# Output projection and second feed-forward projection as 2x2 blocks in seven products of sums

## The chip, the cores and the metric

The kernel runs on one core of a Trainium2 chip. The metric is the device time in microseconds of one execution, from the first to the last instruction and what the launch puts around them. The engines have names of their own in the profile: PE is TensorE (PEld its weight loads), DVE is VectorE, ACT is ScalarE, POOL is GpSimd, SP is SyncE, which here only issues loads and stores.

## The reference

One layer of an encoder with 512 tokens and 1024 features, all in float32:

```python
h = x @ w_in                       # columns: q | k | v | latents | rope key | gate A | gate B
y_a = neighbourhood_attention_2d(q, k, v, rpb) @ w_branch_na      # 8 heads
y_b = latent_attention(q_lat, kv_lat, k_rope, ...) @ w_branch_mla # 8 heads
merged = sigmoid(g_a + b_a) * y_a + sigmoid(g_b + b_b) * y_b
x = layer_norm(DN_ALPHA * x + merged @ w_out, ln1_g, ln1_b)       # (512,1024) @ (1024,1024)
gate, up = split(x @ w_ffn_in)                                    # 2 x 2816 columns
x = layer_norm(DN_ALPHA * x + (silu(gate) * up) @ w_ffn_out, ln2_g, ln2_b)   # (512,2816) @ (2816,1024)
```

The change concerns the two products `merged @ w_out` and `(silu(gate) * up) @ w_ffn_out`, and through its memory the parts between them.

## The kernel before, in words

**Precision.** A float32 operand is kept as two tiles, a rounded part `hi` (ScalarE copies it, L79) and the remainder `lo` (VectorE subtracts, L80); together they are one "split". A product is then three matmuls in a row, hi by hi, hi by lo, lo by hi (`mm3`, L102 to L104). The left operand has 128 contraction rows and 128 tokens, the right one 128 contraction rows and up to 512 columns.

**Stages in program order.** Latents and attentions with other projections between them; gate A, branch A and the merge (L580 to L596); the output projection (L682) with its layer norm and the transposes of the result (L693, split in L701 and L702); the first feed-forward part (22 hidden units of 128, L719 to L732); the second projection with the last layer norm and the stores (L735).

**A projection** (`project_out`, L601) has the eight accumulators of its 512 x 1024 result in the eight PSUM banks (`ACC`, L599): four row blocks of 128 tokens, called 0 to 3 below, by two halves of 512 columns. It goes over the contraction blocks `k` (8 in the output projection, 22 in the second); each block's weights (128 x 1024, 512 KB) are loaded by SyncE into one of two buffers `raw` and split into `hi` and `lo` of 512 columns, of which there are four each; then follow 24 matmuls. The last blocks (`tail`: 4 and 6) are kept back and done row block by row block (L622 to L634), so that the row blocks are complete one after another. Some blocks of the tail are split earlier, into slots of their own (`early`; `V` tiles in the output projection, `X` tiles in the second). The last 256 columns of the last row block have an accumulator of their own.

**The norm** (`residual_norm`, L644) adds the accumulators to the residual rows (L647), takes mean and variance (L655, L657), has 1/sqrt computed on GpSimd (L127, L129), and applies scale and shift in two operations for each half (L660, L664). The residual rows sit in eight tiles `OT`; GpSimd loads them (L674) and multiplies them by ALPHA (L675) while the projection runs, and once more after the transposes (L705).

**What sets the order.** The program is written in the order of the stages, and a scheduler of the framework arranges each engine's instructions anew when the program is built; on the chip each engine runs its own list strictly in order and waits by semaphores. SyncE and GpSimd issue their transfers in that order too. Tiles come from rings (`BUFS`, L64): a tile's name is its ring, so a new `raw` waits until the readers of the `raw` two back are done.

## Time and profile before

| What | Value |
|---|---|
| Time, median of 3 runs | 742.45 us (740.47, 742.45, 743.89) |
| Span of the profiled execution | 739.6 us |
| Granted clock of TensorE, mean over the span | 0.998 |
| Attentions up to the output projection | 0 to 322.9 us, PE busy 317.19 |
| Output projection | 322.9 to 366.4 us |
| Last norms, transposes, first unit of the feed-forward | 366.4 to 382.9 us |
| First feed-forward part, other units | 382.9 to 611.4 us |
| Second projection, up to the last matmul | 611.4 to 731.5 us |
| Last norm and stores | 731.5 to 739.6 us |

The span runs from the first to the last instruction of one execution that the profiler recorded; the time of a run also holds what lies around the span, so the two differ by a few microseconds, and runs differ among themselves. In the rows that follow, an entry such as `lo<-raw,hi 128x512` reads: tile `lo` written from tiles `raw` and `hi`, 128 partitions by 512 elements; `x144` is the number of instructions in a group, behind it their busy time in us and the mean of one in ns, and behind the second bar the idle time of the engine just before them with what ended most of it. A row of the timeline begins with its start and its duration in us, and ends with the wait ahead of it in square brackets.

### The profile page before, as it was taken

The page shows a single profiled execution, that of the slowest core. Times are in us where ns is not written, and L with a number is a line of the kernel's source. Part 1 is how long each engine was busy: PE and PEld are TensorE (multiplying, and loading weights), DVE is VectorE, ACT ScalarE, POOL GpSimd, SP SyncE. Part 2 cuts the span into 40 slices and gives each one's busy share as a digit, 9 for nine tenths or more (in the row PEclk, how much of TensorE's full clock was granted, in tenths as well). Part 3 has the DMA queues.
Part 4 walks back from the last instruction along what each step waited for, and adds up shares of the span by engine and source line. Part 5 has one row for each costly group of instructions (what it writes and reads, how often), then busy time and mean ns, then how long its engine had stood idle before and what let it go on. Part 6 is the DMA issues. An engine that isn't in the chain of part 4 may idle for free.

```text
span 739.6 us, 9589 instructions
## 1 busy us (share of the span) xinstructions
PE 725.1 (98%) x3606; PEld 610.9 (83%) x3606; DVE 390.6 (53%) x649; ACT 313.0 (42%) x608; POOL 106.6 (14%) x214
## 2 busy tenths in 40 slices
PE   8999999999999999999999999999999999999995
PEld 7988888886898788888798888888888888888884
DVE  5657667667847847454973333344334334322265
ACT  5567657667655654332143333333333333322200
POOL 0312211324404340040320000000000000000011
PEclk9999999999999999999999999999999999999999
DMA  7311030113314252266022323323233234432111
GB/s 262 134 58 56 32 101 30 57 48 103 108 58 139 90 185 86 85 204 195 0 86 86 112 88 92 109 86 111 88 97 103 86 109 150 144 111 86 57 50 65
DMA packets 22207, 72.91 MB, mean 99 GB/s; under 512 B 2833, under 2 KB 3729, under 8 KB 22161
## 3 DMA queue, kind: packets, MB, share of 16 engines
q1 hardware_dynamic: 20880, 68.11, 29.3%
q0 software_dynamic: 1280, 4.20, 1.8%
q8 instruction: 28, 0.46, 0.3%
q14 instruction: 19, 0.15, 0.1%
HBM read 70.20 MB, written 2.10 MB: 98 GB/s over the span
## 4 chain that ended last, share of the span: by engine, by line
PE 90%; DVE 4%; POOL 2%; ACT 1%; issue 1%; DMA 1%; SPq 0%; POOLq 0%; DVEq 0%; ACTq 0%
PE psA L103 22%; PE psA L104 22%; PE psA L102 22%; PE psS L104 3%; PE psS L102 3%; PE psS L103 3%; PE psT L426 2%; PE psT L103 2%; PE psT L102 2%; PE psT L104 2%; POOL Q L503 1%; PE psV L438 1%; PE psV L439 1%; PE psV L103 1%; PE psV L102 1%
## 5 line engine op out<-in xcount | busy, mean ns | idle before, releaser
L80 DVE TENSOR_TENSOR lo<-raw,hi 128x512 fp32r<-128x512 f32 (+1 forms) x214 | 148.6, 700 | 207.5 <-ACT hi L79 206.3
L79 ACT ACTIVATE hi<-raw 128x512 fp32r<-128x512 f32 (+1 forms) x214 | 133.3, 628 | 258.0 <-PE psA L103 130.0
L102 PE MATMUL psA<-X,hi 128*128 128x512 f32 (+1 forms) x560 | 217.3, 388 | 0.0
L103 PE MATMUL psA<-X,hi 128*128 128x512 f32 (+1 forms) x560 | 215.3, 384 | 0.0
L104 PE MATMUL psA<-X,lo 128*128 128x512 f32 (+1 forms) x560 | 215.3, 384 | 0.0
L104 PEld LDWEIGHTS psA<-X,lo 128*128 128x128 f32 x560 | 105.3, 188 | 20.5
L103 PEld LDWEIGHTS psA<-X,hi 128*128 128x128 f32 x560 | 105.5, 188 | 19.0
L102 PEld LDWEIGHTS psA<-X,hi 128*128 128x128 f32 x560 | 105.5, 188 | 18.8
L127 POOL TENSOR_SCALAR s<-s 128x1 f32<-128x1 f32 (+1 forms) x12 | 5.4, 453 | 378.6 <-DVE s L657 378.3
L503 POOL TENSOR_SCALAR Q<-SP,s 64x192 f32<-64x192 f32 (+2 forms) x64 | 34.5, 539 | 44.8 <-DVE s L497 40.3
L415 POOL TENSOR_SCALAR SP<-SP,s 128x512 f32<-128x512 f32 x32 | 24.3, 759 | 82.1 <-DVE s L414 80.8
L175 DVE SCALAR_TENSOR_TENSOR PT<-psT,PT 128x512 fp32r<-128x512 f32 (+1 forms) x48 | 31.1, 662 | 5.6 <-ACT PT L174 5.5
L729 DVE TENSOR_TENSOR M<-M,psA 128x512 f32<-128x512 f32 x22 | 15.1, 688 | 34.1 <-PE psA L104 32.4
L174 ACT ACTIVATE PT<-psT 128x512 fp32r<-128x512 f32 (+1 forms) x48 | 26.9, 578 | 13.7 <-PE psT L426 6.2
L412 ACT ACTIVATE SP<-psS,s 128x512 f32<-128x512 f32 x32 | 22.0, 688 | 10.9 <-DVE s L409 10.9
L102 PE MATMUL psA<-OT,hi 128*128 128x512 f32 x64 | 25.6, 400 | 0.0
L104 PE MATMUL psA<-OT,lo 128*128 128x512 f32 x64 | 25.0, 391 | 0.0
L103 PE MATMUL psA<-OT,hi 128*128 128x512 f32 x64 | 25.0, 390 | 0.0
L409 DVE TENSOR_REDUCE s<-psS 128x1 f32<-128x512 f32 x32 | 21.7, 680 | 0.6 <-PE psS L104 0.3
L372 DVE TENSOR_TENSOR M<-psV,M 64x512 f32<-64x512 f32 x16 | 11.0, 689 | 18.8 <-ACT M L371 18.7
L102 PE MATMUL psA<-hi,X 128*128 128x256 f32 (+1 forms) x56 | 18.1, 326 | 0.7 <-ACT hi L79 0.7
L371 ACT ACTIVATE M<-psV 64x512 f32<-64x512 f32 x16 | 9.5, 594 | 21.1 <-PE psV L531 15.6
(434 smaller groups left out, 1251.3 us busy)
## 6 DMA issues: line engine op xcount, KB each, us to landing
raw<-in_wfi_dram SPq DMA_DIRECT2D x44, 512.0 KB, 3.6
raw<-in_wfo_dram SPq DMA_DIRECT2D x22, 512.0 KB, 3.6
raw<-in_wgb_dram SPq DMA_DIRECT2D x8, 512.0 KB, 3.4
raw<-in_wqk_dram SPq DMA_DIRECT2D x8, 512.0 KB, 3.3
raw<-in_wga_dram SPq DMA_DIRECT2D x8, 512.0 KB, 3.4
raw<-in_wout_dram SPq DMA_DIRECT2D x8, 512.0 KB, 4.2
B<-in_nabias_dram SPq DMA_DIRECT2D x8, 384.0 KB, 3.1
raw<-in_wv_dram SPq DMA_DIRECT2D x4, 512.0 KB, 3.5
```

What stands on the lines that cost most here:

```text
L79: act.activation(hi, raw, AF.Copy)
L80: dve.tensor_tensor(out=lo, in0=raw, in1=f(hi), op=ALU.subtract)
L102: pe.matmul(o, lhsT=ah, rhs=bh, start=first, stop=False)
L103: pe.matmul(o, lhsT=ah, rhs=bl, start=False, stop=False)
L104: pe.matmul(o, lhsT=al, rhs=bh, start=False, stop=last)
L174: act.activation(hi, psv, AF.Copy if isinstance(scale, float) else AF.Identity, scale=scale)
L175: dve.scalar_tensor_tensor(out=lo, in0=psv, scalar=scale, in1=f(hi), op0=ALU.mult, op1=ALU.subtract)
L409: dve.reduce_max(out=mx, in_=s, axis=AX.X, negate=True)
L412: act.activation(pr[:, :512], s, AF.Exp, bias=mx, accum_out=sm)
L415: pool.tensor_scalar(out=pr[:, :512], in0=pr[:, :512], scalar1=rc, scalar2=0.0, op0=ALU.mult, op1=ALU.add)
L503: pool.tensor_scalar(out=pr[m_, dst:dst + c1 - c0], in0=ev[m_, i, c0:c1], scalar1=rc[m_, i:i + 1], scalar2=0.0, op0=ALU.mult, op1=ALU.add)
L729: dve.tensor_tensor(out=sg, in0=sg, in1=os[1], op=ALU.mult)
```

## The change

Two contraction blocks and the two halves of the rows and of the columns make a product of 2x2 blocks. `A11, A12` are the rows 256 to 511 of the left operand in contraction block 0 and 1 of a pair, `A21, A22` the rows 0 to 255; `B11, B12, B21, B22` are the weights of 128 x 512 (first index the contraction block, second the column half). Instead of eight block products, seven are made, from sums of blocks:

- 1: A11 B11, and into the same accumulator A12 B21
- 5: (A21 - A22) (B11 + B12), and into the same accumulator (A12 - A11 + A21 - A22) B22
- 7: (A11 - A21) (B12 + B22), and into the same accumulator A22 (B11 + B12 + B22 + B21)
- 6: (A11 - A21 + A22) (B11 + B12 + B22)

The additions at the end give each product its sign. Every product has two row blocks of 128, so four products in each of two row blocks fill the eight banks (`acc`).

The work of a projection is done in three sweeps over the pairs (4 in the output projection, 11 in the second). **Sweep 1** makes the first four products above. For each pair it loads 1 MB into one of two buffers `w` (the weights lie in memory as `B11 | B12 | B22 | B21`), splits the two left sums (`ca`, `cb`) and `B11`, and lets GpSimd make three sums: `t13` (L651, 1024 columns, split into `u13`), `t2` (L654, split into `u2`), and the sum of all four, which overwrites the left sums that are used up (L657). Between sweeps 1 and 2, corrections are added from the accumulators into the residual tiles (L665 to L674). **Sweep 2** adds A22 by the sum of all four to product 7, after which row blocks 0 and 1 are complete and get their norm. **Sweep 3** loads `B22 | B21` once more and finishes products 1 and 5 with the row blocks 2 and 3; the last 2 or 4 pairs are held back and done row block by row block.

The sums of the left blocks are made by VectorE (`combine`, four operations of 256 columns for each pair). The merged values and the hidden units are therefore kept unsplit. All tiles whose rings belong to the attentions are given back behind the merge (`first.close()`), and a second set of rings (`w`, `x0`, `x1`, `rw`) takes their place.

```diff
-    BUFS = dict(raw=2, hi=4, lo=4, X=8, QK=12, V=6, PT=10, SP=6, OT=10, G=8, M=3, Q=4, B=2, s=24, t=3)
+    BOTH = dict(raw=2, hi=4, lo=4, X=8, OT=10, G=8, M=3, s=24, t=3)
+    PHASES = (dict(QK=12, V=6, PT=10, SP=6, Q=4, B=2), dict(w=2, x0=11, x1=11, rw=4))
...
-        dve.tensor_tensor(out=g, in0=g, in1=gates[fc], op=ALU.add)
-        mh = st("QK", [P, T], F32R)
-        ml = st("PT", [P, T], F32R)
-        split(g, mh, ml)
-        merged.append((mh, ml))
+        dve.tensor_tensor(out=gates[fc], in0=g, in1=gates[fc], op=ALU.add)
+        merged.append(gates[fc])
+    first.close()
+    pools.append(ctx.enter_context(tc.tile_pool(name="second", bufs=1, reuse_waits="tile")))
...
+    def combine(a11, a12, a21, a22, s1, s3, s2):
+        dve.tensor_tensor(out=s1, in0=a21, in1=a22, op=ALU.subtract)
+        dve.tensor_tensor(out=s3, in0=a11, in1=a21, op=ALU.subtract)
+        dve.tensor_tensor(out=s2, in0=a11, in1=s1, op=ALU.subtract)
+        dve.tensor_tensor(out=a21, in0=a12, in1=s2, op=ALU.subtract)
...
+        for j, (c1, a22, a12, s4) in enumerate(pairs):
+            w = st("w", [P, 2048])
+            nc.sync.dma_start(out=w, in_=src[j])
+            ca = split_new(ctag, c1[:, 0:512], 512)
+            cb = split_new(ctag, c1[:, 512:1024], 512)
+            b11 = st("hi", [P, 512], F32R), st("lo", [P, 512], F32R)
+            split(w[:, 0:512], *b11)
+            t13 = st("raw", [P, 1024])
+            pool.tensor_tensor(out=t13, in0=w[:, 0:1024], in1=w[:, 512:1536], op=ALU.add)
+            u13 = split_new(wtags[0], t13, 1024)
+            t2 = st("M", [P, 512])
+            pool.tensor_tensor(out=t2, in0=w[:, 0:512], in1=t13[:, 512:1024], op=ALU.add)
+            u2 = st("hi", [P, 512], F32R), st("lo", [P, 512], F32R)
+            split(t2, *u2)
+            pool.tensor_tensor(out=c1[:, 0:512], in0=t2, in1=w[:, 1536:2048], op=ALU.add)
+            parts = [(1, (ca, 0), (b11, 0)), (5, (ca, 256), (u13, 0)), (7, (cb, 0), (u13, 512)), (6, (cb, 256), (u2, 0))]
+            for q, a, b in parts if j < n - 1 else [parts[i] for i in (2, 0, 1, 3)]:
+                for i in range(2):
+                    product(q, i, a, b, j == 0, j == n - 1, False)
+        for i in range(2):
+            r1, r2 = res[2 + i], res[i]
+            dve.scalar_tensor_tensor(out=r2[1], in0=acc[7][i], scalar=-scale, in1=r2[1], op0=ALU.mult, op1=ALU.add)
+        for i in range(2):
+            r1, r2 = res[2 + i], res[i]
+            n1 = st("M", [P, 512])
+            act.activation(n1, acc[1][i], AF.Copy, scale=scale)
+            dve.scalar_tensor_tensor(out=r2[1], in0=acc[5][i], scalar=scale, in1=r2[1], op0=ALU.mult, op1=ALU.add)
+            dve.scalar_tensor_tensor(out=n1, in0=acc[6][i], scalar=scale, in1=n1, op0=ALU.mult, op1=ALU.subtract)
+            dve.tensor_tensor(out=r2[0], in0=r2[0], in1=n1, op=ALU.subtract)
+            pool.tensor_tensor(out=r2[1], in0=r2[1], in1=n1, op=ALU.add)
+            pool.tensor_tensor(out=r1[1], in0=r1[1], in1=n1, op=ALU.add)
...
+            ca = split_new(ctag, a22, 256)
+            u4 = st("hi", [P, 512], F32R), st("lo", [P, 512], F32R)
+            split(c1[:, 0:512], *u4)
+            for i in range(2):
+                product(7, i, (ca, 0), (u4, 0), False, j == n - 1, True)
+        for i in range(2):
+            rows_done(i, [(acc[7][i], 0, 512)], False)
...
+            w = st("w", [P, 1024])
+            nc.sync.dma_start(out=w, in_=src[j][:, 1024:2048])
+            b = split_new(wtags[1] if j < n - tail else wtags[2], w, 1024)
...
+    project_out(mpairs, wout, 0.5, xres, 2, "x1", ("x0", "x0", "x0"), norm1)
...
-        hi, lo = h_slot(j)
-        split(sg, hi, lo)
-        hT.append((hi, lo))
+        if j % 2 == 0:
+            x0 = st("x0", [P, 1280])
+            dve.tensor_tensor(out=x0[:, 0:512], in0=sg, in1=os[1], op=ALU.mult)
+        else:
+            xb = st("x1", [P, 512])
+            dve.tensor_tensor(out=xb, in0=sg, in1=os[1], op=ALU.mult)
+            a22, a12 = xb[:, 0:256], xb[:, 256:512]
+            combine(x0[:, 256:512], a12, x0[:, 0:256], a22, x0[:, 512:768], x0[:, 768:1024], x0[:, 1024:1280])
+            hpairs.append((x0[:, 256:1280], a22, a12, x0[:, 0:256]))
...
+    project_out(hpairs, wfo, 1.0, x1, 4, "G", ("X", "X", "x0"), norm2)
```

The split is L85 and L86 in the changed program, the norm L733 to L751, the residual loads and their scaling L770 and L771, the transposes and their splits L799 and L800. Three places of the new order matter later.

On GpSimd, at the start of the output projection, the residual rows `OT` were loaded and scaled with nothing else between them:

```order
L674 DMA OT_3651<-in_xr_dram 128x512
L674 DMA OT_3654<-in_xr_dram 128x512
L674 DMA OT_3657<-in_xr_dram 128x512
L674 DMA OT_3660<-in_xr_dram 128x512
L675 TENSOR_SCALAR OT_3651<-OT_3651 128x512
L675 TENSOR_SCALAR OT_3654<-OT_3654 128x512
L674 DMA OT_3663<-in_xr_dram 128x512
L675 TENSOR_SCALAR OT_3657<-OT_3657 128x512
L675 TENSOR_SCALAR OT_3660<-OT_3660 128x512
```

Now GpSimd's list has the sums of weights there too (`x_3620` is the sum of all four of pair 0, `M_3755` and `w_3735` are of pair 1):

```order
L654 TENSOR_TENSOR M_3755<-w_3735,raw_3749 128x512
L770 DMA OT_3650<-in_xr_dram 128x512
L770 DMA OT_3653<-in_xr_dram 128x512
L770 DMA OT_3656<-in_xr_dram 128x512
L770 DMA OT_3659<-in_xr_dram 128x512
L771 TENSOR_SCALAR OT_3650<-OT_3650 128x512
L771 TENSOR_SCALAR OT_3653<-OT_3653 128x512
L770 DMA OT_3662<-in_xr_dram 128x512
L771 TENSOR_SCALAR OT_3656<-OT_3656 128x512
L771 TENSOR_SCALAR OT_3659<-OT_3659 128x512
L770 DMA OT_3665<-in_xr_dram 128x512
L657 TENSOR_TENSOR x_3620<-M_3704,w_3684 128x512
```

Six loads and four scalings of the residual stand ahead of the L657 that is the last reader of pair 0's weights `w_3684`, whose buffer pair 2 gets.

On VectorE, in the output projection, the norm of the first row block (`OT_3645`, `OT_3648`) came behind all splits of weights:

```order
L80 TENSOR_TENSOR lo_3846<-raw_3839,hi_3845 128x512
L80 TENSOR_TENSOR lo_4080<-raw_4077,hi_4079 128x512
L80 TENSOR_TENSOR lo_4084<-raw_4077,hi_4083 128x512
L647 SCALAR_TENSOR_TENSOR OT_3645<-psS_3677,OT_3645 128x512
L655 BN_STATS t_3875<-OT_3645 128x6
L647 SCALAR_TENSOR_TENSOR OT_3648<-psS_3678,OT_3648 128x512
```

Now the norms of row blocks 0 and 1 (`OT_3644` to `OT_3653`) stand behind sweep 2, with splits of sweep 3 after them (`x_3995` is a left operand of its first pair, `x_4015` the weights of its second):

```order
L744 BN_AGGR s_3978<-t_3974 128x2
L86 TENSOR_TENSOR x_3995<-G_716,x_3994 128x256
L747 SCALAR_TENSOR_TENSOR OT_3650<-OT_3650,s_3978,rw_3668 128x512
L747 SCALAR_TENSOR_TENSOR OT_3653<-OT_3653,s_3978,rw_3670 128x512
L751 SCALAR_TENSOR_TENSOR OT_3650<-OT_3650,s_3982,rw_3672 128x512
L751 SCALAR_TENSOR_TENSOR OT_3653<-OT_3653,s_3982,rw_3674 128x512
L86 TENSOR_TENSOR x_4015<-w_4012,x_4014 128x1024
```

The split that sweep 3 needs for its second pair comes last of these rows.

On VectorE, at the end of sweep 1 of the second projection (`X_6449`, `G_6435` and `lo_6455` belong to the last pair, `X_6712` and `X_6736` are weights of sweep 3, `G_6528` is a left operand of the third pair of sweep 2):

```order
L86 TENSOR_TENSOR lo_6455<-M_6452,hi_6454 128x512
L86 TENSOR_TENSOR lo_6504<-x_4306,hi_6503 128x512
L86 TENSOR_TENSOR G_6500<-x_4380,G_6499 128x256
L86 TENSOR_TENSOR X_6712<-w_6709,X_6711 128x1024
L86 TENSOR_TENSOR X_6736<-w_6733,X_6735 128x1024
L665 SCALAR_TENSOR_TENSOR OT_3647<-psV_5918,OT_3647 128x512
L665 SCALAR_TENSOR_TENSOR OT_3653<-psA_5919,OT_3653 128x512
...
L672 TENSOR_TENSOR OT_3644<-OT_3644,M_6485 128x512
L672 TENSOR_TENSOR OT_3650<-OT_3650,M_6492 128x512
L86 TENSOR_TENSOR G_6528<-x_4684,G_6527 128x256
```

Two splits of weights for sweep 3 stand ahead of the first correction, which reads accumulator 7 (`psV_5918`, `psA_5919`), and ten rows with all corrections ahead of `G_6528`. Before, this stretch held nothing but splits of `raw`, all alike.

## The prediction

> **What bounds the kernel now.** I read the page first, then the stretches of the span, then the order of time on TensorE, GpSimd and VectorE.

> ```profile
> span 739.6 us, 9589 instructions
> PE 725.1 (98%) x3606; PEld 610.9 (83%) x3606; DVE 390.6 (53%) x649; ACT 313.0 (42%) x608; POOL 106.6 (14%) x214
> PE 90%; DVE 4%; POOL 2%; ACT 1%; issue 1%; DMA 1%; SPq 0%; POOLq 0%; DVEq 0%; ACTq 0%
> ...
> core 0: us, PE busy (x) PEld busy (x) DVE busy (x) ACT busy (x) POOL busy (x), PEclk, DMA share, GB/s
> 322.90:366.40 43.50, 42.97 (x198) 35.26 (x197) 29.29 (x43) 11.00 (x17) 13.47 (x20) 1.00 0.48 156
> 366.40:382.90 16.50, 16.34 (x126) 15.47 (x125) 12.82 (x21) 6.75 (x11) 5.38 (x8) 1.00 0.14 41
> 382.90:611.40 228.50, 228.50 (x1011) 189.19 (x1010) 85.80 (x127) 76.98 (x128) 0.00 (x0) 1.00 0.32 99
> 611.40:731.50 120.10, 120.06 (x547) 99.98 (x545) 48.03 (x71) 24.85 (x38) 4.43 (x6) 1.00 0.31 97
> 731.50:739.60 8.10, 0.00 (x0) 0.00 (x0) 4.07 (x8) 0.00 (x0) 1.69 (x2) 0.79 0.18 65
> ```

> TensorE is busy 98% of the span and is 90% of the chain that ended last. The stretches are the output projection, its last norms with the transposes, the first feed-forward part, the second feed-forward projection, and the tail. In the two projections TensorE never stands still, while VectorE works 67% and 40% of the time and GpSimd 31% and 4%. So a matmul removed there is worth its full step, as long as the others keep feeding TensorE.

> **What is removed.**

> ```profile
> 611.39 0.39 PE L102 MATMUL psS<-hi,G 128*128 128x512 f32 x1
> ...
> 726.76 0.39 PE L104 MATMUL psA<-hi,SP 128*128 128x512 f32 x1
> ```

> From the first to the last of these 510 matmuls of 512 columns pass 115.37 us, so one costs 0.2267 us. Eight products become seven: 192 matmuls become 168 in the output projection, and 528 become 462 in the second (counted in full widths). That is 90 x 0.2267 = **20.4 us** less. It is certain that they go: TensorE's row count falls from 3604 to 3508, the other 6 being narrower pieces at the end.

> **What is added, and its prices.** Each pair of contraction blocks now needs three sums on GpSimd (L651 of 1024 columns, L654 and L657 of 512), five splits on ScalarE and VectorE in the first sweep instead of four, and a 1 MB load into one of two buffers `w`, which comes free only when L657 has run.

> ```profile
> L346 POOL TENSOR_TENSOR Q<-M 128x128 f32<-128x128 f32 x4 | 1.8, 460 | 0.0
> L305 POOL TENSOR_TENSOR kro<-kt,kt 128x64 f32<-128x64 f32 x1 | 0.3, 324 | 0.0
> L705 POOL TENSOR_SCALAR OT<-OT 128x512 f32<-128x512 f32 x8 | 4.8, 622 | 3.5 <-PE psT L693 3.5
> ...
> B<-in_nabias_dram SPq DMA_DIRECT2D x8, 384.0 KB, 3.1
> raw<-in_wqk_dram SPq DMA_DIRECT2D x8, 512.0 KB, 3.3
> raw<-in_wfo_dram SPq DMA_DIRECT2D x22, 512.0 KB, 3.6
> ...
> L79 ACT ACTIVATE X<-raw 128x1024 fp32r<-128x1024 f32 x4 | 4.2, 1061 | 4.7 <-DMA raw<-in_wfo_dram 4.7
> L80 DVE TENSOR_TENSOR X<-raw,X 128x1024 fp32r<-128x1024 f32 x4 | 4.9, 1224 | 3.7 <-ACT X L79 3.7
> L80 DVE TENSOR_TENSOR lo<-raw,hi 128x512 fp32r<-128x512 f32 x206 | 144.0, 704 | 204.0 <-ACT hi L79 202.9 <-PE psA L103 0.6
> ```

> No wide sum of two tensors on GpSimd is in the trace. Bounds: 0.62 us for 512 columns, as the one-input L705, and 1.28 us by the two small sums (64 more columns cost 136 ns, so 460 + 384 x 2.13 ns; 2.37 us for 1024). I take the upper end, the nearer operation. For 1 MB the bounds are 3.6 us (size free) and 5.6 us (0.5 us for each further 128 KB, the first and last load row); 384 to 512 KB by the middle row costs 0.2, which makes 4.4; I take 5.0.

> VectorE and GpSimd also stand in each other's way:

> ```profile
> 326.97 1.33 DVE L80 TENSOR_TENSOR V<-raw,V 128x1024 fp32r<-128x1024 f32 x1 [1.97 <-ACT V L79]
> 328.22 1.10 DVE L80 TENSOR_TENSOR PT<-M,QK 128x512 fp32r<-128x512 f32 x1
> ...
> 321.09 2.13 POOL L674 DMA_DIRECT2D OT<-in_xr_dram  x4 [50.71 <-PE psA L104]
> 327.77 2.04 POOL L675 TENSOR_SCALAR OT<-OT 128x512 f32<-128x512 f32 x2
> 329.75 0.58 POOL L674 DMA_DIRECT2D OT<-in_xr_dram  x1
> ```

> The first L675 is ready at 327.77 and the split ends at 328.30; the next split then takes 1.10 us instead of 0.69, and the two L675 together 2.04 instead of 1.24. They ran in turn, not together. [...]

> The change puts 2.37 + 2 x 1.28 = 4.9 us of GpSimd sums beside 1.22 + 4 x 0.70 = 4.0 us of such splits in each pair.

> **The terms, all beside TensorE.** Steps of 0.2267 us, so pair 0 and 1 of a first sweep last 10.9 us.

> A. *Output projection, first sweep.* In GpSimd's new order L657 of pair 0 stands behind six loads of the residual and four scalings. These wait for the last reader of their slots (321.09 above) and end at 330.33. L657 then ends at 331.6; buffer `w` reloads until 336.6; L651 of pair 2 ends at 339.0, its split at about 342. TensorE is through pairs 0 and 1 at 333.8. Pair 3 repeats it: its L651 follows two more sums and two splits, and the sweep ends near 353.7 instead of 344.7: **9 us** (6.5 without exclusion, 3 with the cheap prices, 11 at most).

> B. *Its second and third sweep.* VectorE has the norms of row blocks 0 and 1 in its queue ahead of the split of the third sweep's second weights.

> ```profile
> 355.54 0.27 PE L693 MATMUL psS<-ident,OT 128*128 128x128 f32 x1
> 355.65 0.27 PE L693 MATMUL psT<-ident,OT 128*128 128x128 f32 x1
> ...
> 364.06 0.68 DVE L647 SCALAR_TENSOR_TENSOR OT<-psA,OT 128x512 f32<-128x512 f32 x1
> ...
> 374.38 1.41 DVE L664 SCALAR_TENSOR_TENSOR OT<-OT,s,SP 128x512 f32<-128x512 f32 x2
> ```

> Two norms with two other splits fill 11.7 us here. After the change some 9.5 us of it lies behind the second sweep's last matmul and ahead of that split; TensorE has 16 matmuls and 12 transposes (0.11 us from one to the next) meanwhile, 4.9 us. **5 us** (3 to 7, the upper end with the corrections of the second sweep blocked by GpSimd's adds).

> C. *Row blocks 2 and 3.* Before, they ended one after the other, 24 matmuls or 5.4 us apart; now their accumulators end within 4 matmuls. Two norms (11.7), transposes and first split (1.5), less 0.9 of those matmuls and 48 half-width matmuls of the feed-forward's first half (5.8 us): **6.5 us** (5 to 8). A half-width matmul costs 0.12 us:

> ```profile
> 729.14 0.28 PE L102 MATMUL psS<-X,V 128*128 128x256 f32 x1
> ...
> 731.18 0.28 PE L104 MATMUL psS<-hi,SP 128*128 128x256 f32 x1
> ```

> These are 17 steps in 2.04 us. The stretch 366.40:382.90 shows only 0.2 us idle now.

> D. *Second projection up to its second sweep.* Two pairs go round in 5.0 (load) + 2 x 2.37 + 2 x 1.28 = 12.3 us, against 10.9 on TensorE, or 14 with the splits that GpSimd lets past. The first `w` free lands about 1.6 us after TensorE enters the stage, so L651 of pair 10 ends at 53 to 61. Behind it, in VectorE's new order (shown with the change), the first correction from accumulator 7 stands after two splits of third-sweep weights, and the load for one of these goes into the buffer that L657 of pair 10 frees: splits 3.6, L657 1.3, a load of 512 KB 3.6, two ScalarE copies 2.1, a VectorE split 1.2 and the correction 0.7, together 12.5. TensorE may touch accumulator 7 only then, at 66 to 73, and would be free at 59.9. I take **8 us**, nearer the lower end, since VectorE waits for ScalarE in part of each round (2 with cheap sums, 13 at most).

> E. *Start of its second sweep.* Ten corrections and splits (6.9 us, at 0.6 to 0.7) stand ahead of the split that the third pair needs; TensorE has 2.7 us of work from the first of them on, and 0.5 more. GpSimd's four adds then alternate with the next splits. **5 us** (3 to 6).

> F. *Tail.*

> ```profile
> 734.58 1.54 DVE L664 SCALAR_TENSOR_TENSOR OT<-OT,s,B 128x512 f32<-128x512 f32 x3 [0.44 <-POOL s L129]
> ```

> Now VectorE ends 4.7 us after TensorE (734.58 + 1.54, less 731.18 + 0.28). After the change row block 2 is complete only 22 matmuls (2.7 us) before the end, so its norm lies in the tail as well: VectorE ends about 8.9 us after. **4 us** (2 to 5).

> The rest I cost at nothing: the sums of the merged values and of the hidden units (four VectorE operations of 256 columns per pair) lie in stretches where TensorE holds 10.9 us per unit pair and VectorE is busy 38%; the splits that they replace go. The new loads move 0.5 MB more per pair at 97 GB/s in that stretch.

> **Sum.** 9 + 5 + 6.5 + 8 + 5 + 4 = 37.5 us of new waits, less 20.4: **+17.1 us**. The span was 739.6, so 756.7; the median of the runs shown lies 2.85 above that span, so **759.5**. All lower ends together are 18 (740.1), all upper ends 50 (772).

> **Rivals.** (1) *GpSimd is cheap* and the preparation runs ahead. If a 1024-column sum takes under about 1.3 us (one-input price doubled, 2 x 0.62) and loads 3.6, two pairs go round in 7.3 us, D vanishes, A falls to 3, E to 2; with B 3, C 5, F 2 that is 15 - 20.4 = -5.4: **737**, faster. For it: GpSimd idles 86% of the span. Against it: the sums in the trace cost 2.13 ns a column.
> (2) *TensorE never waits*: **722**. C speaks against it, since two norms of measured length cannot be hidden by 5.8 us of matmuls.
> (3) *The clock falls in the new pauses.* In the tail, where TensorE is idle, the granted clock is 0.79, and the first matmuls ran at half pace:

> ```profile
> 1.19 3.59 PE L111 MATMUL psT<-M 128*128 128x512 bf16 x8 [1.19 <-DVE M L108]
> ```

> That is 0.43 us each, 1.6 us lost over 8. Five pauses of over 3 us (A twice, C, D, E) would add 8: **768**. [...]
> That the products are not removed is excluded by the row count.

> **How the numbers follow.** Forecast 0.70, rival (1) 0.15, (2) 0.05, (3) 0.10. About 0.5% (3.7 us) is what a measurement of this kernel can tell from no change. Faster by more: (2) and most of (1), 0.16; within: the rest of (1) and the lowest corner of the forecast, 0.08; slower 0.76. The range goes from all lower ends, 740, to all upper ends with part of (3), 773, and leaves out (2), a piece of (1) and of (3), some 0.2.

> **What would show it.** A: TensorE idle at 333.8, released by the split of L651's sum. C: a pause of over 5 us before the second half of the first feed-forward unit. D and E: idle time of TensorE on accumulator 7, released by VectorE, and L651 near 2.4 us. F: VectorE ending 8 to 9 us after TensorE. A granted clock below 1.00 after a pause would be (3). The prediction is wrong if TensorE still is over 97% busy in the two projections, or if L651 takes under 1.3 us.

## The result

The changed kernel took **786.93 us** (median of 4 runs, 785.4 to 788.57) against 741.87 us before (4 runs in the same session): a ratio of 1.0611, 95% interval 1.0586 to 1.0636, so 45 us slower. The forecast was 759.5 us with a range up to 773: the sign was right, the size was not. The profiled execution spans 786.8 us, 47.2 more than before.

The head of the page of the changed kernel, and its row of the granted clock over 40 slices:

```profile
span 786.8 us, 9759 instructions
PE 730.6 (93%) x3510; PEld 605.6 (77%) x3510; DVE 510.1 (65%) x789; ACT 349.9 (44%) x683; POOL 205.8 (26%) x267
PEclk9999999999999999989889999999999998998897
```

The matmuls went as promised (3606 to 3510 in the profile), but TensorE is no longer busy all the time (98% before, 93% now), VectorE has 120 us more, GpSimd twice as much, and the clock is below full in two places. The stretches of the changed kernel, in the columns of the same view before; they are the first sweep of the output projection, its two other sweeps, the last norms with the first feed-forward unit, the other units, the three sweeps of the second projection, and the tail:

```profile
324.46:357.35 32.89, 26.32 (x97) 20.14 (x96) 29.84 (x27) 12.31 (x20) 19.57 (x17) 0.90 0.52 174
357.35:382.65 25.30, 19.91 (x81) 14.48 (x80) 25.30 (x39) 9.19 (x18) 11.99 (x10) 0.93 0.24 80
382.65:405.98 23.33, 18.45 (x124) 17.43 (x123) 17.24 (x30) 6.13 (x10) 7.97 (x14) 0.85 0.46 139
405.98:634.48 228.50, 228.50 (x1010) 189.19 (x1009) 92.49 (x152) 67.64 (x112) 11.69 (x6) 1.00 0.32 93
634.48:719.97 85.49, 70.72 (x265) 53.91 (x264) 70.42 (x59) 35.35 (x56) 55.26 (x28) 0.90 0.38 129
719.97:742.47 22.50, 17.15 (x67) 13.73 (x67) 22.20 (x37) 11.06 (x26) 6.02 (x4) 0.85 0.12 41
742.47:774.79 32.32, 31.05 (x145) 25.07 (x143) 24.98 (x45) 12.64 (x23) 2.39 (x4) 1.00 0.39 129
774.79:786.80 12.01, 0.00 (x1) 0.00 (x0) 7.95 (x17) 0.00 (x0) 2.86 (x4) 0.59 0.24 87
```

Set against 0.2267 us for each matmul of 512 columns, 0.12 for one of 256 and 0.11 for a transpose, the losses are: the first sweep of the output projection 11.1 us (and it starts 1.6 us later than before, which may be no more than profiles differ by: in run 5 below, whose output projection is the same, it starts at 322.3 us), its other sweeps 9.1, the norms with the first feed-forward unit 8.0, the other units none, the second projection 25.6, 7.5 and 2.1 in its sweeps. The tail is 3.9 us longer than before. That is 68.9 us; less the 1.5 us which the same sum gives for before, and less the 20.4 us of matmuls that went, it is 47.0, and the spans differ by 47.2.

Two things show in the rows themselves. The largest loss is the first sweep of the second projection. There TensorE waits, in the order of its waits, for remainders of weights and left sums that VectorE makes:

```profile
PE psS L110 <- DVE lo L86: 5.1, 3, 2.6
PE psS L111 <- DVE G L86: 2.6, 2, 2.3
PE psV L111 <- DVE G L86: 2.1, 1, 2.1
```

(These are the longest rows of waits by line: in all, how many, the longest.) All rows of this view come to 14.7 us, far less than 25.6, because most of the longer pauses cost a second time. The timeline of TensorE behind the wait of 2.25 us:

```profile
662.45 0.80 PE L111 MATMUL psS<-hi,G 128*128 128x512 f32 x1 [2.25 <-DVE G L86]
663.05 0.63 PE L109 MATMUL psS<-hi,G 128*128 128x512 f32 x1
663.48 0.63 PE L110 MATMUL psS<-lo,G 128*128 128x512 f32 x1
663.90 0.63 PE L111 MATMUL psS<-hi,G 128*128 128x512 f32 x1
```

The steps are 0.43 us instead of 0.2267: half pace, for 3.5 to 5.3 us after such a pause. Summed over all matmuls that follow without a wait, from their start times, this is 19.7 us: 8.8 up to the first feed-forward unit and 10.9 in the second projection.

Why VectorE is late is seen in its groups and GpSimd's over the same sweep (busy, mean of one in ns, idle time before):

```profile
L651 POOL TENSOR_TENSOR raw<-w 128x1024 f32<-128x1024 f32 x9 | 24.8, 2759 | 5.3 <-DVE lo L86 3.0 <-DMA w<-in_wfo_dram 2.3
L86 DVE TENSOR_TENSOR G<-x,G 128x512 fp32r<-128x512 f32 x18 | 20.7, 1162 | 0.0
L657 POOL TENSOR_TENSOR x<-M,w 128x512 f32<-128x512 f32 x10 | 18.6, 1865 | 15.5 <-DVE G L86 15.5
L86 DVE TENSOR_TENSOR lo<-M,hi 128x512 fp32r<-128x512 f32 x10 | 15.6, 1557 | 0.0
L654 POOL TENSOR_TENSOR M<-w,raw 128x512 f32<-128x512 f32 x9 | 14.3, 1593 | 0.4
```

A split of 512 columns that took 0.70 us before takes 1.2 to 1.6 now, and the sums are lengthened too. One round of two pairs in GpSimd's timeline:

```profile
653.76 2.84 POOL L651 TENSOR_TENSOR raw<-w 128x1024 f32<-128x1024 f32 x1
656.67 1.29 POOL L654 TENSOR_TENSOR M<-w,raw 128x512 f32<-128x512 f32 x1
658.97 2.88 POOL L651 TENSOR_TENSOR raw<-w 128x1024 f32<-128x1024 f32 x1 [1.01 <-DMA w<-in_wfo_dram]
662.54 1.29 POOL L657 TENSOR_TENSOR x<-M,w 128x512 f32<-128x512 f32 x1 [0.69 <-DVE G L86]
663.79 2.26 POOL L654 TENSOR_TENSOR M<-w,raw 128x512 f32<-128x512 f32 x1
667.95 1.61 POOL L657 TENSOR_TENSOR x<-M,w 128x512 f32<-128x512 f32 x1 [1.90 <-DVE G L86]
669.51 2.85 POOL L651 TENSOR_TENSOR raw<-w 128x1024 f32<-128x1024 f32 x1
```

From one L651 to the second next 15.75 us pass, with the following rounds 16.5 and 16.1; TensorE needs 10.9 for two pairs. Without a neighbour the sums take what the prediction said: 1.29 us for 512 columns, 2.35 to 2.45 for 1024.

### The profile page after: what moved, and what is told of

Same layout as the page of the kernel before. It is cut to its first block, busy times and chain, and to the rows that moved or that the text cites. A ratio compares the mean times of both kernels' runs of the same rounds, so it can differ in the third digit from the quotient of the medians.

```text
span 786.8 us, 9759 instructions
## 1 busy us (share of the span) xinstructions
PE 730.6 (93%) x3510; PEld 605.6 (77%) x3510; DVE 510.1 (65%) x789; ACT 349.9 (44%) x683; POOL 205.8 (26%) x267
## 5 line engine op out<-in xcount | busy, mean ns | idle before, releaser
L111 PE MATMUL psA<-X,lo 128*128 128x512 f32 (+1 forms) x560 | 216.4, 387 | 1.3 <-DVE lo L86 1.3
L86 DVE TENSOR_TENSOR lo<-raw,hi 128x512 fp32r<-128x512 f32 (+1 forms) x168 | 117.0, 699 | 132.5 <-ACT hi L85 132.0
L85 ACT ACTIVATE hi<-raw 128x512 fp32r<-128x512 f32 (+1 forms) x168 | 105.1, 627 | 199.2 <-PE psA L110 164.5
L111 PEld LDWEIGHTS psA<-X,lo 128*128 128x128 f32 x560 | 106.3, 190 | 22.4 <-DVE lo L86 1.6
L651 POOL TENSOR_TENSOR raw<-w 128x1024 f32<-128x1024 f32 x15 | 40.1, 2672 | 263.7 <-DVE lo L86 258.1
L86 DVE TENSOR_TENSOR G<-x,G 128x256 fp32r<-128x256 f32 (+1 forms) x55 | 37.0, 700 | 0.0
L657 POOL TENSOR_TENSOR x<-M,w 128x512 f32<-128x512 f32 x15 | 26.4, 1763 | 15.7 <-DVE G L86 15.5
L85 ACT ACTIVATE G<-x 128x256 fp32r<-128x256 f32 (+1 forms) x55 | 25.2, 490 | 8.5 <-PE psT L110 3.0
L85 ACT ACTIVATE X<-raw 128x1024 fp32r<-128x1024 f32 x11 | 11.7, 1059 | 35.9 <-POOL raw L651 35.8
L109 PE MATMUL psA<-OT,hi 128*128 128x512 f32 x64 | 25.6, 400 | 0.0
L111 PE MATMUL psA<-OT,lo 128*128 128x512 f32 x64 | 25.0, 391 | 0.0
L654 POOL TENSOR_TENSOR M<-w,raw 128x512 f32<-128x512 f32 x15 | 23.7, 1587 | 0.5
## 6 DMA issues: line engine op xcount, KB each, us to landing
raw<-in_wfi_dram SPq DMA_DIRECT2D x44, 512.0 KB, 3.6
w<-in_wfo_dram SPq DMA_DIRECT2D x11, 512.0 KB, 3.7
raw<-in_wgb_dram SPq DMA_DIRECT2D x8, 512.0 KB, 3.3
raw<-in_wqk_dram SPq DMA_DIRECT2D x8, 512.0 KB, 3.3
raw<-in_wga_dram SPq DMA_DIRECT2D x8, 512.0 KB, 3.3
B<-in_nabias_dram SPq DMA_DIRECT2D x8, 384.0 KB, 3.1
```

The source lines that it names most:

```text
L85: act.activation(hi, raw, AF.Copy)
L86: dve.tensor_tensor(out=lo, in0=raw, in1=f(hi), op=ALU.subtract)
L109: pe.matmul(o, lhsT=ah, rhs=bh, start=first, stop=False, skip_group_check=go_on)
L111: pe.matmul(o, lhsT=al, rhs=bh, start=False, stop=last, skip_group_check=go_on)
L651: pool.tensor_tensor(out=t13, in0=w[:, 0:1024], in1=w[:, 512:1536], op=ALU.add)
L654: pool.tensor_tensor(out=t2, in0=w[:, 0:512], in1=t13[:, 512:1024], op=ALU.add)
```

## The experiments

Beside these runs the kernel before had medians of 741.1 us (runs 1 to 4), 741.22 (5 to 8) and 740.56 (9 to 11). Where no interval is given there was one timed run; the stretches are read from one profile each.

**1. The sums on VectorE.** In both projections:

```diff
-            pool.tensor_tensor(out=t13, in0=w[:, 0:1024], in1=w[:, 512:1536], op=ALU.add)
+            dve.tensor_tensor(out=t13, in0=w[:, 0:1024], in1=w[:, 512:1536], op=ALU.add)
```

and the same for the other two sums.

> The three sums of each pair are made by VectorE instead of GpSimd, in both projections. Theory (GpSimd's sums and VectorE's splits exclude each other, so that their times add up): alone, a pair costs 2.37 + 2 x 1.29 = 4.9 us of GpSimd and 1.22 + 4 x 0.68 = 3.9 us of VectorE, 8.9 us together against 5.44 us of TensorE; with the sums on VectorE it is 3.9 + 1.2 + 2 x 0.68 = 6.5 us. The first sweep of the second projection falls from 85.5 to 68 to 73 us, that of the output projection from 32.9 to 25 to 28 us, the whole to 763 to 771 us; splits of 512 columns take 0.68 us each. Rival (the engines run side by side, VectorE is not what is late): VectorE gets 2.6 us of work more per pair and the time stays or rises, 785 to 800 us. Rival (the clock after pauses makes the loss): pauses stay, since VectorE has more to do; over 780 us.

765.86 us, ratio to before 1.0338 (1.0321 to 1.0356). The stretches of this kernel from its output projection to the second feed-forward unit, and the first two sweeps of the second projection:

```profile
321.41:402.62 81.21, 64.21 (x298) 51.89 (x296) 66.50 (x100) 27.54 (x48) 31.30 (x33) 0.87 0.40 136
631.12:691.57 60.45, 60.26 (x265) 49.39 (x264) 60.25 (x86) 35.22 (x54) 0.00 (x0) 1.00 0.47 157
691.57:714.50 22.93, 17.89 (x67) 14.22 (x66) 20.58 (x32) 10.84 (x24) 6.04 (x4) 0.85 0.06 13
```

The first sweep went from 85.5 to 60.5 us, TensorE's own pace, with VectorE busy for 60.25 of them: the theory's direction, and more than it gave. Its 6.5 us per pair were too many, since VectorE's instructions start 0.60 us apart where one takes 0.68. Both rivals fall. In the output projection the first sweep fell as the theory had it, from 32.9 to 27.3 us, but the stretch behind it, up to the second feed-forward unit, grew from 48.6 to 53.9 us, so that the whole stretch, the first row, hardly moved (81.5 us before the edit). The whole time came out in its range only because two errors cancel: the second projection gained more than forecast, the output projection nothing.

**2. The sums left out.**

```diff
-            t13 = st("raw", [P, 1024])
-            pool.tensor_tensor(out=t13, in0=w[:, 0:1024], in1=w[:, 512:1536], op=ALU.add)
-            u13 = split_new(wtags[0], t13, 1024)
+            u13 = split_new(wtags[0], w[:, 512:1536], 1024)
```

> The three sums of each pair are left out in both projections; the splits take the weights as they are loaded. Theory (sums and splits add up): 3.9 us of splits per pair lie under 5.44 us of TensorE, so the first sweeps go at TensorE's pace: 60 to 63 us in the second projection, 22 to 24 us in the output projection, the whole 750 to 757 us. What is left above 722 is the corrections, the norms and the tail. Rival (loads into two buffers of 1 MB are late): the first sweep stays over 70 us, with waits that end on loads. Rival (the splits alone are too much for VectorE): the same, with waits that end on VectorE.

760.5 us, above the expected 750 to 757. The second projection's first sweep took 59.8 us, as expected. The output projection's first sweep went at pace as well (22.2 us), but the whole stretch up to the second feed-forward unit fell only to 78.95 us: 4.8 us of wait came up at the second pair of the second sweep instead, behind the corrections, and the norms kept theirs. What was gained in the first sweep was lost behind it.

**3. Fills in place of sums.**

```diff
-            pool.tensor_tensor(out=t2, in0=w[:, 0:512], in1=t13[:, 512:1024], op=ALU.add)
+            pool.tensor_tensor(out=t2[:, 0:8], in0=w[:, 0:8], in1=t13[:, 512:520], op=ALU.add)
+            for _ in range(3):
+                pool.memset(t2[:, 8:512], 0.01)
```

> Each sum on GpSimd is made over 8 columns only, and the rest of its result is filled by three fills in a row, which write and read nothing; the splits on VectorE stay as they are. Theory (it is the reads of two tensors that exclude each other): VectorE's splits take 0.68 us beside the fills, the first sweep of the second projection falls to 60 to 66 us, the whole to 750 to 762 us, although GpSimd is still busy in it. Rival (any GpSimd instruction keeps VectorE out): splits stay near 1.2 to 1.8 us beside the fills and the time stays above 772 us. Rival (only GpSimd's own length counts): the time goes with GpSimd's busy time, whatever the splits take.

767.34 us. The first sweep of the second projection, in the columns of the stretches:

```profile
632.83:698.14 65.31, 61.00 (x266) 49.09 (x264) 41.33 (x59) 35.48 (x57) 53.26 (x106) 1.00 0.49 162
```

VectorE's groups of splits in it:

```profile
L86 DVE TENSOR_TENSOR G<-x,G 128x512 fp32r<-128x512 f32 x18 | 12.2, 685 | 0.8 <-ACT G L85 0.8
L86 DVE TENSOR_TENSOR lo<-M,hi 128x512 fp32r<-128x512 f32 x10 | 6.8, 684 | 0.0
```

GpSimd is as busy as in the changed kernel (53.3 us against 55.3), yet every split takes 0.685 us and the sweep falls by 20 us. So it is the sums' reading that keeps VectorE out, not GpSimd being busy. The 5.5 us that are left over TensorE's pace were not taken apart. The whole missed its expectation by 5 us, again in the output projection (82.3 us).

**4. Seven products in the second projection only.** The output projection of before (its `project_out`, splits of the merged values and weights by rows) with the second projection of the change.

> The output projection is as before the change, with eight products; only the second projection has seven. Theory (each stage pays for itself): the output projection and what follows it lost 29.8 us and saved 5.4, so the whole is 787 - 24 = 763 us (759 to 767), and the second projection's three sweeps take 85, 22 and 32 us as in the changed kernel. Rival (the new memory layout or the load of the changed output projection slows the rest): the second projection's sweeps change by more than 3 us.

767.15 us, at the edge of the range and 20 less than the changed kernel (21.5 in the spans), where 24 were expected: the second projection began 22.4 us earlier, and its last matmuls took 1.2 us longer. The first sweep took 85.2 us, the second 22.2, the third 33.5. Each projection loses by itself; they do not harm each other.

**5. Zero matmuls in the pauses.**

```diff
+            if tail > 2 and j > 0:
+                for i in range(4):
+                    for c in range(0, 512, 128):
+                        pe.matmul(acc[1][i % 2][:, c:c + 128], lhsT=blank[:, 0:128], rhs=blank[:, 128:256], start=False, stop=False, skip_group_check=True)
```

> The changed kernel with 16 matmuls of zeros (128 columns, bf16) ahead of each pair but the first in the first sweep of the second projection: TensorE pauses less long there, so that its clock stays up; they take 1 to 2 us of TensorE per pair and add nothing to the result. Theory (sums and splits, 8.9 us a pair when they exclude each other, set the pace): the first sweep stays at 83 to 88 us though the granted clock in it rises from 0.90 to over 0.96; the whole stays at 783 to 790 us. Rival (half clock after each pause makes much of the loss): the sweep falls by up to 12 us, what its waits don't cover, the whole to 774 to 780 us.

793.97 us; the sweep got longer, 93.4 us, though the clock in it rose to 0.95:

```profile
633.03:726.47 93.44, 78.22 (x426) 59.53 (x424) 61.42 (x61) 35.97 (x58) 52.51 (x28) 0.95 0.36 124
```

In TensorE's timeline the zero matmuls and the first matmul behind them:

```profile
661.49 1.07 PE L664 MATMUL psS<-swap 128*128 128x128 bf16 x16
662.36 0.48 PE L109 MATMUL psS<-hi,G 128*128 128x512 f32 x1
```

Sixteen of them cost 0.87 us, 8.7 in ten pairs, and the sweep grew by 8. The rival's forecast falls, and the theory's too: were TensorE only waiting for sums and splits, the zero matmuls would have been hidden. So TensorE's own time seems to be a link of the loop; which buffer closes it was not tried. What a better clock alone is worth stays open. The half pace shrank by some 4 us (0.10 of 85.5 us against 0.05 of 93.4), while 8.7 us of matmuls came in, and the run does not separate the two.

**6. Residual rows by SyncE and ScalarE.**

```diff
-            nc.gpsimd.dma_start(out=t, in_=xr[tb][:, hf * 512:hf * 512 + 512])
-            pool.tensor_scalar(out=t, in0=t, scalar1=ALPHA, scalar2=0.0, op0=ALU.mult, op1=ALU.add)
+            nc.sync.dma_start(out=t, in_=xr[tb][:, hf * 512:hf * 512 + 512])
+            act.activation(t, t, AF.Copy, scale=ALPHA)
```

> The changed kernel, but the residual rows are loaded by SyncE and scaled by ScalarE instead of GpSimd. Theory (VectorE, with what excludes it, is busy all through the output projection and its norms, 70.1 of 75.5 us): the six loads and eight scalings no longer keep VectorE out, which gives it some 5 us back (0.61 us each) and frees the weights' buffer sooner: the stretch from the first matmul of the output projection to the second feed-forward unit falls from 81.5 to 74 to 78 us, the whole to 779 to 784 us. Rival (the prediction's own step A: only the order on GpSimd delays the weights, 9 us): the first sweep falls from 32.9 to 23 to 26 us and the whole by as much, to 777 to 780 us.

787.51 us: nothing in the whole. The stretch took 83.1 us, so the forecasts of theory and rival both miss. But the first sweep did move:

```profile
322.41:351.68 29.27, 24.82 (x98) 18.92 (x96) 26.35 (x27) 15.66 (x26) 13.07 (x7) 0.94 0.62 210
```

It took 29.3 us instead of 32.9 (33.4 in run 5, where this part of the program is unchanged). The weights of the third and fourth pair were asked for from 323.1 us on, 0.7 us into the sweep, where the changed kernel asks at 331.5, 7.0 us into it. Behind the first sweep 53.9 us passed instead of 48.6, as in run 1, and took the gain back; why was not taken apart.

**7. Run 4 with run 1's sums.**

> Eight products in the output projection, seven in the second, and its sums on VectorE. Theory (the two parts add up): 767 less the 25 us by which the first sweep fell when the sums moved, 740 to 744 us, the same as before the change within 0.5%: the 15 us of matmuls that the second projection saves are given back by its corrections (8), third sweep (2 to 5) and tail (4 to 5). Rival (the sums on VectorE only moved the work, and it comes back where VectorE is needed next): 746 to 752 us.

743.95 us, ratio 1.0035 (1.0021 to 1.0049): the sums alone decide between 767 and 744. The three sweeps took 60.6, 22.8 and 35.5 us; the rival does not come in the first sweep, though the third is 3 us longer than in the changed kernel.

**8. A mixture.** As run 7, with 16 contraction blocks in seven products and the other six as before: two between the corrections and the second sweep, four at the end, row block by row block. The additions of the corrections are on VectorE as well.

```diff
+        whole(*units[0], True)
...
+        for j in range(m):
+            second(j)
+            if j == 3:
+                whole(*units[1], False)
...
+        for tb in range(NTB):
+            def run(hf, o, c0, width, start):
+                for u, lhs, w in held:
+                    step(u, lhs, w, tb, hf, o, c0, width, start and u == held[0][0], u == held[-1][0], not start)
+            run(0, place(tb, 0), 0, 512, False)
```

Here `whole` multiplies one block in the ordinary way into eight accumulators, two of which are the banks of product 6 taken anew; `second` is a pair of the second sweep, `held` are the last four blocks.

> As the run with eight products in the output projection and the sums on VectorE, but in the second projection only 16 of the 22 contraction blocks go in seven products; the other six are multiplied in the ordinary way, two of them between the corrections and the second sweep, four at the end, row block by row block, as before the change; the four additions of the corrections are on VectorE too. Theory (VectorE's work per matmul is what has to fit): it saves 48 matmuls or 10.9 us; VectorE has 47 us in a first sweep of 43.5, 17 in a second of 21.8 and 20 in a third of 21.8, and the tail is that of before, so 3 to 5 us of waits are left: 733 to 738 us. Rival (corrections stop TensorE whatever stands beside them, 8 us): 740 to 744 us. Rival (VectorE is late all through): over 744 us.

**736.72 us** (735.5 to 737.24), ratio 0.9935 (0.9918 to 0.9952): 0.5 to 0.8% less than the kernel before, a small gain. Its second projection and tail:

```profile
610.00:656.00 46.00, 46.00 (x205) 38.10 (x204) 45.83 (x65) 26.30 (x41) 0.00 (x0) 1.00 0.46 150
656.00:678.00 22.00, 22.00 (x99) 18.22 (x98) 18.59 (x36) 13.48 (x28) 0.00 (x0) 1.00 0.23 69
678.00:700.00 22.00, 19.91 (x82) 14.49 (x81) 11.31 (x20) 10.25 (x19) 0.00 (x0) 1.00 0.56 169
700.00:724.71 24.71, 24.63 (x117) 19.87 (x115) 20.06 (x34) 2.31 (x4) 5.07 (x6) 1.00 0.19 65
724.71:734.60 9.89, 0.01 (x1) 0.00 (x0) 5.87 (x13) 0.00 (x0) 1.68 (x2) 0.68 0.29 106
```

In the first row, which holds the first sweep, VectorE is busy for 45.83 of 46 us and TensorE still never waits; the corrections lie under the ordinary blocks, and the clock stays at 1.00. It saves 10.9 us of matmuls and gives back some 6 (the spans differ by 5.0).

**9. The third sum alone on VectorE** (the L657 of the changed kernel; the other two stay).

> The changed kernel, but the third sum of each pair (512 columns, the one that overwrites the left sums) is on VectorE; the other two stay on GpSimd. Theory (times that exclude each other add up): 8.9 - 1.29 + 0.6 = 8.2 us a pair, 0.7 less for each of the nine pairs behind the first two, so the first sweep of the second projection falls from 85.5 to 78 to 81 us. Rival (GpSimd's list is what is late: the third sum waits there until the left sums are split, 15.5 us in all, and the next pair's sums wait behind it): without that head of the queue GpSimd has 4 to 4.5 us a pair, and the sweep falls to 62 to 70 us.

787.7 us. The first sweep took 80.9 us, in the theory's range and outside the rival's. But GpSimd now waits elsewhere, for loads:

```profile
POOL raw L651 <- DMA w<-in_wfo_dram: 33.5, 7, 7.7
```

The buffer of weights is freed by the sum that moved, then refilled; with two buffers this turn is part of the loop. So the number came out, while "times add up" is not all of it. What the sweep gained was lost in the output projection (85.8 us) and the second sweep (23.8).

**10. The corrections' additions on VectorE**, in run 7's kernel.

> As the run with eight products in the output projection and the sums on VectorE, with the four additions of the second projection's corrections on VectorE too, instead of GpSimd. Theory (GpSimd's adds, 1.3 us each alone, keep the splits of the second sweep out): four adds of 0.6 us instead of 1.3, so the second sweep of the second projection falls from 22.8 to 20 to 21 us, and splits beside it take 0.68. Rival (the ten corrections in a row on VectorE are the wait): it stays or rises, 23 to 25 us.

740.36 us (run 7: 743.95). The second sweep fell from 22.8 to 20.5 us, as the theory had it, and the third from 35.5 to 32.8.

**11. GpSimd out of the way in both projections:** the edits of runs 1, 6 and 10 in the changed kernel.

> The changed kernel with sums and corrections' additions on VectorE, and the residual rows loaded by SyncE and scaled by ScalarE, so that GpSimd has almost nothing left beside VectorE in either projection. Theory for the output projection (VectorE's own work in that stretch and the order of its list set it): the stretch from its first matmul to the second feed-forward unit stays at 76 to 82 us (81.5 in the changed kernel). Rival (there too GpSimd keeps VectorE out): it falls under 70 us. The second projection is as in the run before it, so the whole is 758 to 765 us by the theory.

751.05 us, below the expected 758 to 765. The stretch of the output projection:

```profile
322.25:393.94 71.69, 60.68 (x298) 49.40 (x296) 62.58 (x104) 30.67 (x54) 15.41 (x20) 0.93 0.46 152
```

71.7 us, 10 less than in the changed kernel, between the theory and its rival. Runs 1 and 6 alone bought next to nothing there (81.2 and 83.1 us), the three edits together 10 us; the third, the corrections' additions, was not tried alone in this projection. The first sweep now goes at pace (22.7 us), and behind it 49.0 us pass, not the 53.9 of runs 1 and 6. The other 10.7 us over the same stretch of run 4 (61.0 us, with 24 matmuls more) may lie with VectorE, busy 62.6 us here against 41.6 there, and with the order of its list; this was not taken apart further.

## Why the prediction was right and wrong

**What went** was right: 20.4 us, and VectorE and GpSimd as the engines that TensorE waits for. Rivals (1) and (2) did not come. The prices of the sums were right to 0.1 us (2.37 and 1.28 predicted), and so was the exclusion of sums and splits. Run 3 ties it to the sums' reading: a split took 0.685 us beside fills and 1.2 to 1.6 beside the sums of the changed kernel.

**D failed, and carries most of the miss** (8 us predicted, 13 at most, 25.6 measured). The step: "Two pairs go round in 5.0 (load) + 2 x 2.37 + 2 x 1.28 = 12.3 us, against 10.9 on TensorE, or 14 with the splits that GpSimd lets past". It holds four of the six sums of two pairs, and one allowance of 1.7 us for splits, although the text had just put 4.9 us of sums beside 4.0 us of splits in each pair. By its own prices, if nothing of it overlaps, that is 2 x 8.9 = 17.8 us for two pairs; measured were 15.75 to 16.5. Some 4.5 rounds that are 5.3 us too long make 24. Of the 25.6 us some 8.9 are half pace, so the waits proper are near 17, still twice the forecast. The wait was then placed at accumulator 7 at the end; in the trace only 1.6 us are there (TensorE waiting for L665), and the rest is spread over the sweep, at the first weights and left sums of every second pair. Runs 1, 2 and 3 show that the sums' reads are the cause; runs 5 and 9 indicate that the loop also passes through TensorE and the refill of the buffers.

**The clock failed as a rival.** It was priced once, at 8 us for five pauses of over 3 us, as an alternative to the forecast. No run shows that length as a limit, and it is no alternative: half pace came with the forecast's own pauses, shorter ones too (2.05 and 2.14 us in the first sweep of the second projection), and added up to 19.7 us over all terms. Counted so, the predicted waits of 37.5 us met 47.7 us of waits, with the half pace on top. How much of the half pace lengthens the end is another matter, which run 5 leaves open.

**A** had the size nearly right (9; measured 11.1), and its chain of times came: L657 of pair 0 ended at 331.45 us (331.6 predicted), L651 of pair 2 at 339.46 (339.0). But "L657 of pair 0 stands behind six loads of the residual and four scalings" is only a part of the cause: run 6 took these away, and the first sweep fell by 3.6 us; run 1 moved the sums, and it fell by 5.6; run 11 did both and more, and it fell by 10.2. **B** (5) and **C** (6.5) came out at 9.1 and 8.0, of which 5.4 us are half pace. That A, B and C are one account shows in runs 1, 2 and 6: each shortened the first sweep (by 5.6, 10.7 and 3.6 us), and most or all of it was lost behind. The prediction added stage by stage. Set against the whole stretch, VectorE is busy for 72.4 of 81.5 us in the changed kernel (the three first rows of the stretches); that this is what ties A, B and C together is argued, not shown.

**E** (5; 7.5 measured, 2.0 of it half pace) was right in kind: run 10 took 2.3 us off by moving GpSimd's adds. That the ten corrections in a row hold the rest fits run 8, where ordinary blocks lie beside them and TensorE does not wait, but it was not tried alone. **F** (4) came out at 3.9. The third sweep, **costed at nothing**, lost 2.1. Of the signs that the prediction named, L651's price, E's wait at accumulator 7 (5.3 us, ended by a split of VectorE) and F's (VectorE ends 8.5 us after TensorE) came; C's single pause of over 5 us did not (3.3 us), nor did D's at accumulator 7.

## What to carry to other kernels

Fewer matmuls are worth something only where the engines that prepare their operands have the time: add up their work per unit of TensorE's work, sweep by sweep and over the whole stretch, and where GpSimd's sums and VectorE's splits run in turn, as here (1.2 to 1.6 us for a split of 0.685), add their times. Here seven products paid a little (0.65%), in the second projection alone, once the sums were on one engine and a quarter of the blocks, in the ordinary form, lay beside the corrections and under the end. Half pace, 19.7 us here, belongs to the pauses of a forecast and is not a case apart, though these runs do not say how much of it reaches the end.

## What the runs showed of the hardware

VectorE was kept out over several GpSimd instructions in a row. VectorE's timeline of the changed kernel, and GpSimd's at the same time:

```profile
328.15 6.00 DVE L618 TENSOR_TENSOR x<-G,x 128x256 f32<-128x256 f32 x1
...
328.40 1.21 POOL L771 TENSOR_SCALAR OT<-OT 128x512 f32<-128x512 f32 x2
329.55 0.57 POOL L770 DMA_DIRECT2D OT<-in_xr_dram  x1
330.15 1.30 POOL L657 TENSOR_TENSOR x<-M,w 128x512 f32<-128x512 f32 x1
331.41 0.62 POOL L771 TENSOR_SCALAR OT<-OT 128x512 f32<-128x512 f32 x1
332.00 1.29 POOL L657 TENSOR_TENSOR x<-M,w 128x512 f32<-128x512 f32 x1
333.25 0.61 POOL L771 TENSOR_SCALAR OT<-OT 128x512 f32<-128x512 f32 x1
```

A difference of 256 columns, 0.41 us elsewhere, took 6.00 us and ended 0.29 us after the last of seven GpSimd instructions, which followed each other without a gap; it did not get in between them. In run 5, whose output projection is the same, it took 3.60 us and got in three instructions earlier, so the number is not fixed.

```profile
354.32 0.50 PE L110 MATMUL psV<-lo,x 128*128 128x512 f32 x1 [2.42 <-DVE lo L86]
354.66 0.40 PE L111 MATMUL psV<-hi,x 128*128 128x512 f32 x1
354.89 0.40 PE L109 MATMUL psA<-hi,x 128*128 128x512 f32 x1
...
724.01 0.73 PE L111 MATMUL psS<-X,G 128*128 128x512 f32 x2 [1.79 <-DVE G L86]
...
725.31 0.63 PE L109 MATMUL psS<-X,G 128*128 128x512 f32 x1
725.74 0.63 PE L109 MATMUL psT<-X,G 128*128 128x512 f32 x1
```

Behind the longer pause the matmuls start 0.23 us apart: a border of slots at 352.67 cuts it into 0.77 and 1.65 us. Behind the shorter one they are 0.43 us apart: it lies whole in the slot from 721.31 to 724.72, and the granted clock is 0.50 in the next. Counted from the start and end times of the matmuls in all thirteen traces, each of the 59 slots at full clock with 1.96 us or more of standstill was followed by a half one, 8 of the 16 with 1.65 to 1.96 us, and one of the 2686 with less. In the changed kernel alone these are nine slots with 2.05 us or more, one with 1.68, and the one with less, 1.22 us. So a slot in which TensorE stood still for little more than half of its 3.41 us was enough here.
